# Every tile that the large matmuls read starts at a multiple of 2 KB in SBUF, with a smaller reserve for dynamic DMAs

## The chip, the cores and the metric

The kernel runs on one core of one Trainium2 chip. The metric is the device time of one execution in microseconds; a lower time is better. The time shown is the median of three runs.

## The reference

The reference is one even and one odd layer of an encoder trunk on 512 tokens of 2048 features, in float32, followed by a final RMSNorm. Cut to what matters:

```python
# even layer: one projection, 2048 -> 8192, in eight parts
h = rms_norm(x, g) * (1.0 + scale) + shift            # scale, shift, gate: silu(c) @ w_mod + b_mod
q, k, v, z_a, u_b, g_b, g_c, z_b = split(h @ w_in)
y_a = dilated_mixture_attention(rope(q), rope(k), v) * silu(z_a)   # 8 heads of 128
y_b = g_b * short_conv(g_c * u_b, conv_w) * silu(z_b)
x = x + gate * (concat(y_a, y_b) @ w_out)
# odd layer: 2048 -> 6144
u, v, z = split(h @ w_in)
v = layer_norm(gelu(v))
y = gelu(u) * (w_s @ v + b_s) * silu(z)
x = x + gate * (y @ w_out)
return rms_norm(x, final_g)
```

Nearly all the arithmetic is in four products with weights: 2048 to 8192, 2048 to 2048, 2048 to 6144 and 2048 to 2048, each for 512 tokens.

## The kernel before, in words

Activations lie feature-major: 128 features on the partitions, 512 tokens along the free dimension, so one "page" is 128 x 512 float32, which is 2048 bytes per partition. A product of two float32 operands is made of three float32r matmuls: each operand is split into a high part (a cast to float32r) and a low part (what the cast lost), and `mm3` (lines 209 to 214) adds high x high (L212), high x low (L213) and low x high (L214) into one PSUM bank. In the profile such a line stands as `ps<-moving,stationary`: in `ps<-hh,whi` the moving operand is the activation's high part `hh`, 512 columns, and the stationary one a 128 x 128 piece of the weight's high part `whi`.

There are two ways of use. `fmajor` (L227) makes 128 output features for all tokens: the weights are stationary and the activations `hh`, `lh` move (48 matmuls per output tile). `tmajor` (L249) makes 512 output features for each of four token tiles: pieces of `hh`, `lh` are stationary and the weights `whi`, `wlo` move. `half` (L238) is `fmajor` for 256 tokens, used for the last two output tiles of each output projection. The q k product (`scores`, L412) has the same three matmuls with `hqk`, `lqk` on both sides.

Weights come in slices of 128 x 1024 by DMAs of SyncE's queue (`Stream.ahead`, L183) into `wraw` (three buffers); ScalarE casts a slice to `whi` (L191), VectorE subtracts to `wlo` (L192), two buffers each. A slice feeds 24 matmuls of 512 columns. Up to 180 us the conditioning product `silu(c) @ w_mod` runs on VectorE over 48 tiles (`mod_tile`, L161 to L170) beside the first matmuls.

The order of the work on each engine is that of the program's text as a tile framework schedules it. Tiles come from pools: `const` (allocated first), `work` (all through the kernel: `xy`, `hh`, `R`, `r4`, `tmp`, `wraw`, `whi`, `wlo`, `lh`, `mx`, `den`, laid one after the other), and pools of one phase each (`pm`, `pa`, `pb`, `pw`, `pc`, `pz`) behind it. `r4` (L126), `mx` and `den` (L413, L414) are tiles of 16 bytes per partition with two buffers of 32 bytes each, so `tmp` and what follows lie 64 bytes off the pages ahead of it, and the phase pools another 128 bytes off. The first 16384 bytes of every partition are reserved for dynamic DMAs. What the allocator then gives (bytes in a partition, modulo 512, which is also the length of a stationary piece's row of 128 columns, so that all pieces of a tile share its remainder):

| tiles | read by matmuls as | before: first address, mod 512 | after: first address, mod 512 |
|---|---|---|---|
| `hh` (16) | moving in `fmajor`, stationary in `tmajor` | 52608, 384 | 38912, 0 |
| `lh` (16) | the same | 126400, 448 | 112640, 0 |
| `whi`, `wlo` of `work` (2 + 2) | stationary in `fmajor`, moving in `tmajor` | 110016 and 118208, 448 | 96256 and 104448, 0 |
| `whi`, `wlo` of `pa`, `pw` | the same, up to 200 us and at the change of layers | from 159296, 64 | from 145408, 0 |
| `hqk`, `lqk`, `hpt`, `lpt`, `hv`, `lv` | attention, both sides | from 175680, 64 | from 161792, 0 |
| `p`, `sv`, `wst` | transposes and the odd layer's mixing | from 167488, 64 | from 153600, 0 |
| `ident`, `ones`, `cs` | small matmuls of the norms and transposes | 17376, 17888, 19328: 480, 480, 384 | 2016, 2528, 5440: 480, 480, 320 |

Before, the tiles end at byte 228928; after, at 215040.

Of the kernel before, what the change touches and what calls it, by code (L numbers as in the profile page):

```python
# [9 lines left out]
F32 = mybir.dt.float32  # L10
# [6 lines left out]
P = 128  # L17
KT = D // P
NT = S // P
# [2 lines left out]
EPS = 1e-6  # L22
SCALE = P ** -0.5
HALF = 1024
ALL, LEFT, RIGHT = slice(0, S), slice(0, S // 2), slice(S // 2, S)

# Columns of the packed per-feature vectors.
V_ABB, V_SGB, V_ABG, V_SGG, V_FG, V_CONV, V_LNG, V_LNB, V_C, V_N = 0, 48, 96, 112, 128, 144, 168, 184, 200, 216


def rows(c0):
    """A feature-major tile: 128 columns of a weight, two slices of eight row tiles each."""
    return [[(kt, c0, P) for kt in range(8 * h, 8 * h + 8)] for h in range(2)]


def wide(c0, n):
    """n columns of a weight, row tile after row tile, in slices of 1024 columns."""
    per = HALF // n
    return [[(kt, c0, n) for kt in range(per * i, per * i + per)] for i in range(KT // per)]

# [1 line left out]
A_Q, A_K, A_V, A_Z, B_U, B_GB, B_GC, B_Z = (i * 1024 for i in range(8))  # L42
AB_PLAN = []
W_P = 768
# Columns that are taken while the conditioning arrives, beside the first W_P gates of A.
AB_GROUPS = [
    [(A_V, 512)],
    [(A_Z + W_P, 256), (B_U, P), (B_GC, P)],
# [18 lines left out]
def trunk(ctx, tc, xT, vecs, ab_wm, sg_wm, ab_wp, ab_wg, ab_wi, ab_wo, sg_wi, sg_wo, wsT, bs, rope, band, eye, out):  # L67
    nc = tc.nc
    PS = bass.MemoryType.PSUM
    const = ctx.enter_context(tc.tile_pool(name="const", bufs=1))  # L70
    work = ctx.enter_context(tc.tile_pool(name="work", bufs=2))
# [7 lines left out]
        return (pool or work).tile([P, S], dt, tag=tag, bufs=bufs, name=tag)  # L79

    class Pages:
        """Pages in groups of four, each group one block of memory."""

        def __init__(self):
            self.g = [work.tile([P, 4, S], F32, tag="xy", bufs=4, name="xy") for _ in range(4)]
# [7 lines left out]
    def bank():  # L93
        return psum.tile([P, S], F32, tag="ps", name="ps")

# [1 line left out]
    vec = const.tile([P, V_N], F32, name="vec")  # L97
    pm = tc.alloc_tile_pool(name="pm", bufs=1)
    cb = pm.tile([P, D], F32, name="cb")
# [4 lines left out]
    macc = {n: const.tile([P, 48], F32, name=f"macc_{n}") for n in ("ab", "sg")}  # L104
    gsc = {n: const.tile([P, KT], F32, name=f"gsc_{n}") for n in ("ab", "sg")}

    nc.sync.dma_start(out=vec, in_=vecs)
    nc.sync.dma_start(out=ident, in_=eye)
    x_t = Pages()
# [5 lines left out]
    def v1(c):  # L115
        return vec[:, c:c + 1]

# [1 line left out]
    def rms(parts, cols=ALL):  # L119
        n = (cols.stop - cols.start) // P  # L120
        sums = [bank() for _ in range(n)]
        for j, s in enumerate(parts):
            for i, acc in enumerate(sums):
                ts = slice(cols.start + i * P, cols.start + (i + 1) * P)
                nc.tensor.matmul(acc[:, 0:1], lhsT=s[:, ts], rhs=ones[:, 0:1], start=j == 0, stop=j == len(parts) - 1)  # L125
        r4 = work.tile([P, NT], F32, tag="r4", name="r4")  # L126
        for i, acc in enumerate(sums):
            nc.vector.tensor_scalar(out=r4[:, i:i + 1], in0=acc[:, 0:1], scalar1=1.0 / D, scalar2=EPS, op0=ALU.mult, op1=ALU.add)  # L128
        nc.gpsimd.tensor_tensor(out=r4[:, :n], in0=r4[:, :n], in1=mhalf[:, :n], op=ALU.pow)  # L129
        dg = page("tmp", 4)  # L130
        for i in range(n):
            nc.vector.tensor_scalar(out=dg[:, i * P:(i + 1) * P], in0=ident, scalar1=r4[:, i:i + 1], scalar2=None, op0=ALU.mult)
        return dg
# [9 lines left out]
        nc.scalar.activation(out=sq[:, cols], in_=t[:, cols], func=AF.Square)  # L143
        return sq

# [1 line left out]
    cs = const.tile([P, KT], F32, name="cs")  # L147
    nc.scalar.activation(out=cs, in_=vec[:, V_C:V_C + KT], func=AF.Tanh, scale=0.5)
    nc.vector.scalar_tensor_tensor(out=cs, in0=cs, scalar=1.0, in1=vec[:, V_C:V_C + KT], op0=ALU.add, op1=ALU.mult)
    for i in range(4):  # L150
        acc = bank()
# [23 lines left out]
            out=gsc[n][:, kt:kt + 1], in0=mods[n][:, KT + kt:KT + kt + 1], scalar=1.0, in1=g,  # L175
            op0=ALU.add, op1=ALU.mult)

# [1 line left out]
    class Stream:  # L179
        def __init__(self, src, n):  # L180
            self.src, self.n, self.got, self.at = src, n, {}, 0
# [25 lines left out]
        return hi, lo  # L207

    def mm3(acc, w, m, first, last):
        """acc += w.T m for operands in two parts each; the product of the two low parts is below  # L210
        float32's own rounding of the sum."""
        nc.tensor.matmul(acc, lhsT=w[0], rhs=m[0], start=first, stop=False)  # L212
        nc.tensor.matmul(acc, lhsT=w[0], rhs=m[1], start=False, stop=False)  # L213
        nc.tensor.matmul(acc, lhsT=w[1], rhs=m[0], start=False, stop=last)  # L214
# [10 lines left out]
            return w  # L225

    def fmajor(pos, act):  # L227
        """128 features on partitions, all tokens."""
        acc = bank()
        for h in range(2):  # L230
            hi, lo = pos.slice()
            for k in range(8):
                kt = 8 * h + k
                cs = slice(k * P, (k + 1) * P)
                mm3(acc, (hi[:, cs], lo[:, cs]), act[kt], kt == 0, kt == KT - 1)
        return acc

    def half(parts, act, cols, at=None, meanwhile=None):  # L238
        """A feature-major tile for one half of the tokens."""
        acc = bank()  # L240
        for kt in range(KT):
            hi, lo = parts[kt // 8]
            cs = slice(kt % 8 * P, (kt % 8 + 1) * P)
            mm3(acc[:, cols], (hi[:, cs], lo[:, cs]), (act[kt][0][:, cols], act[kt][1][:, cols]), kt == 0, kt == KT - 1)
            if kt == at:
                meanwhile()
        return acc

    def tmajor(pos, act):  # L249
        """512 features of each token tile, tokens on partitions."""  # L250
        accs = [bank() for _ in range(NT)]
        for i in range(8):
            hi, lo = pos.slice()
            for k in range(2):
                kt = 2 * i + k
                cs = slice(k * S, (k + 1) * S)
                for j, acc in enumerate(accs):
                    ts = slice(j * P, (j + 1) * P)
                    a = act[kt]
                    mm3(acc, (a[0][:, ts], a[1][:, ts]), (hi[:, cs], lo[:, cs]), kt == 0, kt == KT - 1)  # L260
        return accs

    def modulated(n, kt, t, r, to=None, cols=ALL):
        """h = x r g (1 + scale) + shift, in two parts."""
        xr = page("tmp", 4)
        nc.vector.scalar_tensor_tensor(  # L266
            out=xr[:, cols], in0=t[:, cols], scalar=gsc[n][:, kt:kt + 1], in1=r[:, cols], op0=ALU.mult, op1=ALU.mult)
        hi, lo = to or (page("hh", 16, F32R), page("lh", 16, F32R))
        sh = mods[n][:, kt:kt + 1]
        nc.scalar.activation(out=hi[:, cols], in_=xr[:, cols], func=AF.Identity, bias=sh)  # L270
        nc.vector.scalar_tensor_tensor(  # L271
            out=lo[:, cols], in0=xr[:, cols], scalar=sh, in1=hi[:, cols].bitcast(F32), op0=ALU.add, op1=ALU.subtract)
        return hi, lo

    def twice_silu(acc, s):
        """2 silu(z) = (tanh(z/2) + 1) z."""
        nc.scalar.activation(out=s, in_=acc, func=AF.Tanh, scale=0.5)
        nc.vector.scalar_tensor_tensor(out=s, in0=s, scalar=1.0, in1=acc, op0=ALU.add, op1=ALU.mult)
        return s
# [1 line left out]
    s_abi, s_abo = Stream(ab_wi, len(AB_PLAN)), Stream(ab_wo, len(OUT_PLAN))  # L281
    s_sgi, s_sgo = Stream(sg_wi, len(SG_PLAN)), Stream(sg_wo, len(OUT_PLAN))

    # ================= layer 0 =================
    class Later:
        """Conditioning tiles that follow the weights' slices at an even pace."""

        def __init__(self, pool, tiles, slices):
            self.pool, self.tiles, self.step, self.at = pool, tiles, len(tiles) / slices, 0.0
# [14 lines left out]
    h = []  # L304
    pos = Pos(s_abi, s_abo)
    pa = tc.alloc_tile_pool(name="pa", bufs=2, reuse_waits="tile")
    parts = []
# [8 lines left out]
    r0 = page("R", 2)  # L316
    spread(rms(parts[:1]), r0)

    # While the conditioning arrives: the gates of A, half of its values, and what the first head and
    # the first features of B need. Six tiles stay in PSUM; the others are summed in SBUF, quarter of  # L320
    # the features by quarter, four tiles at a time.
    def split_w(src, n, pool, bufs):
        raw = work.tile([P, HALF], F32, tag="wraw", bufs=3, name="wraw")[:, :n]
        size = HALF if pool is work else n
# [7 lines left out]
    gates = [bank() for _ in range(6)]  # L332
    sums, held = {}, {}
# [23 lines left out]
    for kt in range(KT):  # L357
# [11 lines left out]
        if q:  # L369
            at = 4 * (q - 1) + 2 * (i % 2)  # L370
# [39 lines left out]
        return split_to(a, "qk", 2, pb)  # L410

    def scores(q, k):  # L412
        mx = work.tile([P, NT], F32, tag="mx", name="mx")  # L413
        den = work.tile([P, NT], F32, tag="den", name="den")  # L414
        ps = []
        for i in range(NT):
            ts = slice(i * P, (i + 1) * P)
            acc = bank()
# [70 lines left out]
    spill = dram.tile([KT, P, S], F32, name="spill")  # L489

    def project(pos, n, y, src, done, wider, left, more=None):
        """The residual sums, the two last of them by halves of the tokens."""
        yy = [split_to(y[kt], "h", 16) for kt in range(KT)]
        res = Pages()
        for g in range(4):
# [19 lines left out]
        two = [[pos.slice(), pos.slice()] for _ in range(2)]  # L515
# [4 lines left out]
        r = page("R", 2)  # L520
# [9 lines left out]

        return res, r, right

    # The slices that the halves of the tokens go through twice, or far apart.
    h = []

    def done0(f, res):
# [13 lines left out]

    x2, r1, right = project(Pos(s_abo, s_sgi, later), "ab", y, xT, done0, wider0, left0, s_sgi)

    # ================= layer 1 =================
    pos = Pos(s_sgi, s_sgo)
    first = [bank() for _ in range(NT)]
    parts = right()
# [26 lines left out]
    for i in range(2):  # L583
        acc = bank()
# [35 lines left out]
    for f in range(KT):  # L620
        accu = fmajor(pos, h)
        m = mix(f)
# [31 lines left out]


def sliced(w, plan):
    """The slices of a weight in the order of their use, each a block of 128 x 1024."""
    w = w.reshape(KT, P, -1)
    a = np.empty((len(plan), P, HALF), w.dtype)
    for i, parts in enumerate(plan):  # L660
        at = 0
        for kt, c0, n in parts:
            a[i, :, at:at + n] = w[kt, :, c0:c0 + n]
            at += n
    return a
# [61 lines left out]
```

## Time and profile before

| | before |
|---|---|
| median of three runs | 1776.43 us |
| lowest and highest | 1772.96 and 1776.67 us |
| profiled execution, first to last instruction | 1773.5 us |
| TensorE busy | 1719.1 us, 97% |
| VectorE busy | 967.8 us, 55% |
| ScalarE busy | 511.2 us, 29% |
| GpSimd busy | 159.2 us, 9% |
| bytes moved by DMA | 276.10 MB, mean 156 GB/s |

The profiled execution is one of its own; the profile gives its span alone, and the median lies 2.9 us above that. The busy time of TensorE counts a matmul from its start to its modelled end, and consecutive matmuls overlap, so the mean length of a matmul (some 390 ns for 512 columns) is not its cost: in a stream without waits the cost of a matmul is the step from its start to the next one's start. The timeline shows starts to 0.01 us, so a step is read over many matmuls: last start less first start, divided by the count.

### The profile page before, as it was taken

The numbers are of one execution on the slowest core, as the hardware profiler recorded it, in microseconds if no ns is written. First come the engines' busy times: TensorE is split into PE (matmuls) and PEld (weight loads), VectorE is DVE, ScalarE is ACT, GpSimd is POOL, SyncE is SP. The second block draws the span as 40 slices with busy tenths as digits, with TensorE's granted clock in tenths as the row PEclk, the third lists the DMA queues.
The fourth block names the chain that finished last, engine by engine and source line by source line (L and its number), as shares of the span: only waits on it lengthen the run. The fifth ranks groups of instructions, "written<-read, shape, count | busy, mean of one in ns | idle before, by whom it ended". The sixth has DMA issues, their size and how long they took to land.

```text
span 1773.5 us, 19357 instructions
## 1 busy us (share of the span) xinstructions
PE 1719.1 (97%) x7638; PEld 1390.4 (78%) x7638; DVE 967.8 (55%) x1446; ACT 511.2 (29%) x709; POOL 159.2 (9%) x103
## 2 busy tenths in 40 slices
PE   5898999999999999999999999999999999999996
PEld 4677787887888887888888988888888888888885
DVE  7898648565645565657554562226444444453344
ACT  3232234232213232324222432222222122242230
POOL 2574520000000000000000000000000000000002
PEclk7999999999999999999999999999999999999998
DMA  8787444344445444445654522334444434352322
GB/s 307 252 294 258 143 135 132 137 172 156 140 163 189 145 162 159 155 154 188 236 178 171 166 94 74 97 98 135 143 134 140 141 132 142 131 190 95 95 95 95
DMA packets 86971, 276.10 MB, mean 156 GB/s; under 512 B 8800, under 2 KB 13152, under 8 KB 86880
## 3 DMA queue, kind: packets, MB, share of 16 engines
q1 hardware_dynamic: 86880, 274.87, 45.8%
q8 instruction: 59, 0.97, 0.2%
q14 instruction: 32, 0.26, 0.0%
HBM read 266.45 MB, written 8.39 MB: 155 GB/s over the span
## 4 chain that ended last, share of the span: by engine, by line
PE 89%; DVE 8%; issue 2%; ACT 1%; DMA 1%; POOL 0%; SPq 0%; DVEq 0%; POOLq 0%; ACTq 0%
PE ps L212 29%; PE ps L213 29%; PE ps L214 29%; DVE mraw L167 4%; PE ps L610 1%; PE ps L437 1%; DVE gsc_ab L174 1%; DVE lh L271 1%; DVE xy L646 1%; DVE tmp L266 1%; ACT hh L270 0%; DMA mraw<-in_ab_wm_dram 0%; PE ps L125 0%; DMA xy<-in_xT_dram 0%; PE ps L138 0%
## 5 line engine op out<-in xcount | busy, mean ns | idle before, releaser
L212 PE MATMUL ps<-hh,whi 128*128 128x512 f32 (+1 forms) x1984 | 776.7, 393 | 17.0 <-ACT hh L270 12.1
L213 PE MATMUL ps<-lh,whi 128*128 128x512 f32 (+1 forms) x1984 | 778.0, 392 | 0.6 <-DVE lh L271 0.6
L214 PE MATMUL ps<-hh,wlo 128*128 128x512 f32 (+1 forms) x1984 | 768.5, 387 | 1.5 <-POOL wlo L329 1.5
L192 DVE TENSOR_TENSOR wlo<-wraw,whi 128x1024 fp32r<-128x1024 f32 x252 | 308.1, 1224 | 495.1 <-ACT whi L191 439.9
L191 ACT CAST whi<-wraw 128x1024 fp32r<-128x1024 f32 x252 | 264.0, 1049 | 940.6 <-PE ps L213 769.3
L212 PEld LDWEIGHTS ps<-hh,whi 128*128 128x128 f32 x1984 | 373.6, 189 | 110.8 <-ACT hh L270 15.8
L214 PEld LDWEIGHTS ps<-hh,wlo 128*128 128x128 f32 x1984 | 375.4, 189 | 90.2 <-POOL wlo L329 2.3
L213 PEld LDWEIGHTS ps<-lh,whi 128*128 128x128 f32 x1984 | 375.2, 189 | 80.6 <-DVE lh L271 1.4
L212 PE MATMUL ps<-whi,hh 128*128 128x512 f32 x384 | 152.8, 398 | 1.7 <-DVE xy L355 1.6
L213 PE MATMUL ps<-wlo,hh 128*128 128x512 f32 x384 | 150.6, 392 | 0.1
L214 PE MATMUL ps<-whi,lh 128*128 128x512 f32 x384 | 150.3, 391 | 0.0
L167 DVE CUSTOM_DVE_ANT_0 mraw<-mraw,cb,vec 128x1024 f32<-128x1024 f32 x96 | 133.2, 1387 | 30.7 <-DMA mraw<-in_sg_wm_dram 20.1
L329 POOL TENSOR_TENSOR wlo<-wraw,whi 128x512 fp32r<-128x512 f32 (+1 forms) x64 | 119.8, 1894 | 101.1 <-ACT whi L328 99.0
L212 PEld LDWEIGHTS ps<-whi,hh 128*128 128x128 f32 x384 | 72.4, 189 | 19.3 <-DVE xy L355 3.2
L214 PEld LDWEIGHTS ps<-whi,lh 128*128 128x128 f32 x384 | 72.1, 188 | 17.0
L213 PEld LDWEIGHTS ps<-wlo,hh 128*128 128x128 f32 x384 | 72.3, 188 | 16.3 <-POOL wlo L329 0.8
L129 POOL TENSOR_TENSOR r<-r,mhalf 128x2 f32<-128x2 f32 (+1 forms) x5 | 5.7, 1139 | 807.3 <-DVE r L128 807.3
L167 DVE CUSTOM_DVE_ANT_0 mraw<-mraw,cb,macc_ab 128x1024 f32<-128x1024 f32 x48 | 74.3, 1547 | 1.2
L408 POOL TENSOR_TENSOR tmp<-tmp,ropeT 128x512 f32<-128x512 f32 x16 | 20.8, 1302 | 523.5 <-DVE wlo L192 470.5
L328 ACT CAST whi<-wraw 128x512 fp32r<-128x512 f32 (+1 forms) x64 | 42.3, 672 | 86.4 <-DMA wraw<-in_ab_wp_dram 41.5
L167 DVE CUSTOM_DVE_ANT_0 mraw<-mraw,cb,macc_sg 128x1024 f32<-128x1024 f32 x48 | 61.5, 1282 | 3.3 <-DMA mraw<-in_sg_wm_dram 2.0
L501 DVE SCALAR_TENSOR_TENSOR xy<-ps,mod_sg,xy 128x512 f32<-128x512 f32 (+1 forms) x18 | 12.4, 691 | 55.8 <-PE ps L214 55.8
(127 smaller groups left out, 880.0 us busy)
## 6 DMA issues: line engine op xcount, KB each, us to landing
mraw<-in_ab_wm_dram SPq DMA_DIRECT2D x96, 512.0 KB, 4.9
mraw<-in_sg_wm_dram SPq DMA_DIRECT2D x96, 512.0 KB, 5.3
wraw<-in_sg_wi_dram SPq DMA_DIRECT2D x96, 512.0 KB, 3.5
wraw<-in_ab_wi_dram SPq DMA_DIRECT2D x92, 512.0 KB, 3.5
wraw<-in_ab_wo_dram SPq DMA_DIRECT2D x32, 512.0 KB, 3.6
wraw<-in_sg_wo_dram SPq DMA_DIRECT2D x32, 512.0 KB, 3.5
wraw<-in_ab_wg_dram SPq DMA_DIRECT2D x48, 256.0 KB, 2.9
wraw<-in_ab_wp_dram SPq DMA_DIRECT2D x16, 384.0 KB, 4.7
```

The source lines that it names most:

```text
L167: nc.vector.tensor_tensor_reduce(out=raw, in0=raw, in1=cb[:, h * HALF:(h + 1) * HALF], scale=0.5, scalar=v1(b + nt) if h == 0 else macc[n] ...
L174: nc.vector.scalar_tensor_tensor(out=gsc[n][:, kt:kt + 1], in0=mods[n][:, KT + kt:KT + kt + 1], scalar=1.0, in1=g, op0=ALU.add, op1=ALU.mult)
L191: nc.scalar.copy(out=hi, in_=raw)
L192: nc.vector.tensor_tensor(out=lo, in0=raw, in1=hi.bitcast(F32), op=ALU.subtract)
L212: nc.tensor.matmul(acc, lhsT=w[0], rhs=m[0], start=first, stop=False)
L213: nc.tensor.matmul(acc, lhsT=w[0], rhs=m[1], start=False, stop=False)
L214: nc.tensor.matmul(acc, lhsT=w[1], rhs=m[0], start=False, stop=last)
L266: nc.vector.scalar_tensor_tensor(out=xr[:, cols], in0=t[:, cols], scalar=gsc[n][:, kt:kt + 1], in1=r[:, cols], op0=ALU.mult, op1=ALU.mult)
L271: nc.vector.scalar_tensor_tensor(out=lo[:, cols], in0=xr[:, cols], scalar=sh, in1=hi[:, cols].bitcast(F32), op0=ALU.add, op1=ALU.subtract)
L328: nc.scalar.copy(out=hi, in_=raw)
L329: nc.gpsimd.tensor_tensor(out=lo, in0=raw, in1=hi.bitcast(F32), op=ALU.subtract)
L408: nc.gpsimd.tensor_tensor(out=sw, in0=sw, in1=sinT, op=ALU.mult)
```

## The change

It alters where tiles lie, and nothing of what is computed. Three edits do it: the three small tiles `r4`, `mx` and `den` go from `work` to `const`; a tile `pad` of 368 float32 per partition (1472 bytes) closes `const`, so that `work` begins at 6144, a multiple of 2048; and the reserve for dynamic DMAs is given as 1024 bytes where it was 16384. `pad` has one MEMSET of 128 x 1 on GpSimd, since a tile has to be written. The rest of the diff takes out comments and docstrings; line numbers after them are four higher in the changed kernel. On every engine the instructions stand in the same order with the same waits as before, but for that one MEMSET.

```diff
+PAD = 368
...
+    pad = const.tile([P, PAD], F32, name="pad")
+    nc.gpsimd.memset(pad[:, 0:1], 0.0)
     nc.sync.dma_start(out=vec, in_=vecs)
...
-        r4 = work.tile([P, NT], F32, tag="r4", name="r4")
+        r4 = const.tile([P, NT], F32, tag="r4", bufs=2, name="r4")
...
-        mx = work.tile([P, NT], F32, tag="mx", name="mx")
-        den = work.tile([P, NT], F32, tag="den", name="den")
+        mx = const.tile([P, NT], F32, tag="mx", bufs=2, name="mx")
+        den = const.tile([P, NT], F32, tag="den", bufs=2, name="den")
...
-    nc = bacc.Bacc("TRN2", target_bir_lowering=False, num_devices=1)
+    nc = bacc.Bacc("TRN2", target_bir_lowering=False, num_devices=1, dynamic_dma_scratch_size=1024)
```

## Rows read from the trace of the kernel before

**Rows 1.** The page: TensorE's busy row, its granted clock by slices, the chain's shares.

```profile
PE 1719.1 (97%) x7638; PEld 1390.4 (78%) x7638; DVE 967.8 (55%) x1446; ACT 511.2 (29%) x709; POOL 159.2 (9%) x103
...
PEclk7999999999999999999999999999999999999998
...
PE 89%; DVE 8%; issue 2%; ACT 1%; DMA 1%; POOL 0%; SPq 0%; DVEq 0%; POOLq 0%; ACTq 0%
```

**Rows 2.** Busy time by stretches: length; PE, PEld, DVE, ACT, POOL; clock; DMA share; GB/s.

```profile
167.70:172.30 4.60, 4.60 (x12) 3.63 (x11) 3.30 (x6) 0.72 (x1) 0.00 (x0) 0.50 0.96 363
...
200.00:1000.00 800.00, 799.55 (x3513) 644.28 (x3513) 456.56 (x717) 243.30 (x344) 38.90 (x30) 1.00 0.48 162
...
721.13:723.63 2.50, 2.50 (x13) 2.06 (x12) 1.62 (x3) 1.53 (x2) 0.00 (x0) 1.00 0.90 369
...
1200.00:1700.00 500.00, 500.00 (x2202) 403.33 (x2202) 227.42 (x330) 129.91 (x156) 1.84 (x1) 1.00 0.40 133
```

**Rows 3.** Waits: the longest of the weights' path (us in total, times, longest).

```profile
ACT whi L191 <- PE ps L213: 769.3, 185, 5.9
```

**Rows 4.** Matmuls by line and shape, 200 to 1700 us: count, busy us, mean ns.

```profile
L212 PE MATMUL ps<-hh,whi 128*128 128x512 f32 x1663 | 663.1, 399 | 0.0
L213 PE MATMUL ps<-lh,whi 128*128 128x512 f32 x1662 | 661.5, 398 | 0.0
L214 PE MATMUL ps<-hh,wlo 128*128 128x512 f32 x1663 | 652.9, 393 | 0.0
L212 PE MATMUL ps<-whi,hh 128*128 128x512 f32 x336 | 132.8, 395 | 0.0
```

**Rows 5.** TensorE's timeline in `fmajor`: start, length, operation; last row 24 matmuls on.

```profile
605.55 0.40 PE L212 MATMUL ps<-hh,whi 128*128 128x512 f32 x1
605.79 0.40 PE L213 MATMUL ps<-lh,whi 128*128 128x512 f32 x1
606.03 0.39 PE L214 MATMUL ps<-hh,wlo 128*128 128x512 f32 x1
...
611.18 0.40 PE L212 MATMUL ps<-hh,whi 128*128 128x512 f32 x1
```

**Rows 6.** The same in `tmajor`, weights at remainder 448; the rows are 45 matmuls apart.

```profile
1100.23 0.39 PE L212 MATMUL ps<-whi,hh 128*128 128x512 f32 x1
...
1110.53 0.39 PE L212 MATMUL ps<-whi,hh 128*128 128x512 f32 x1
```

**Rows 7.** Token-major matmuls, weights at remainder 64 (`pw`); 12 matmuls apart.

```profile
1051.66 0.40 PE L212 MATMUL ps<-whi,hh 128*128 128x512 f32 x1
...
1054.43 0.40 PE L212 MATMUL ps<-whi,hh 128*128 128x512 f32 x1
```

**Rows 8.** The q k product of one head; first and last of its 12 matmuls.

```profile
721.13 0.39 PE L212 MATMUL ps<-hqk 128*128 128x512 f32 x1
...
723.63 0.40 PE L214 MATMUL ps<-hqk,lqk 128*128 128x512 f32 x1
```

**Rows 9.** The q k product of another head; first and last of its 12 matmuls.

```profile
303.35 0.40 PE L212 MATMUL ps<-hqk 128*128 128x512 f32 x1
...
305.89 0.40 PE L214 MATMUL ps<-hqk,lqk 128*128 128x512 f32 x1
```

**Rows 10.** `fmajor`-shaped matmuls at half the granted clock; 11 matmuls apart.

```profile
167.70 0.63 PE L213 MATMUL ps<-lh,whi 128*128 128x512 f32 x1
...
172.39 0.63 PE L212 MATMUL ps<-hh,whi 128*128 128x512 f32 x1
```

**Rows 11.** `half` (256 columns); the rows are 28 matmuls apart.

```profile
1015.02 0.28 PE L213 MATMUL ps<-lh,whi 128*128 128x256 f32 x1
...
1018.32 0.28 PE L214 MATMUL ps<-hh,wlo 128*128 128x256 f32 x1
```

**Rows 12.** DMA queues of the page: packets, MB, share of 16 engines.

```profile
q1 hardware_dynamic: 86880, 274.87, 45.8%
```

**Rows 13.** The nearest MEMSET of GpSimd: min/median/max ns, start in us.

```profile
L113 POOL MEMSET mhalf<- x1: 105/105/105, 0.7 to 0.7; 128x8 f32 x1
```

## The prediction, made before the changed kernel ran

> **What bounds the kernel now.** I read the page first: its busy row, the clock by slices and the shares of the chain [rows 1]. The reader is to see TensorE at 97%, its clock granted in full in nearly all slices, and 89% of the chain on it. Then the busy time by stretches [rows 2]: from 200 to 1000 us TensorE works 799.55 of 800 us and from 1200 to 1700 us all 500, with VectorE under 60% and the DMAs at 40 to 48%. So from 200 us to the tail the time is the number of matmuls times the step from one start to the next. Before that it is not: in the stretch at 167.7 us VectorE works 3.30 of 4.60 us, the DMAs are at 0.96 and the clock at half. The waits say that the weights are early: ScalarE waited 769.3 us for TensorE to give back `whi` [rows 3].
>
> The step itself comes from the timeline, last start less first start over the count. Feature-major matmuls of 512 columns make 24 steps from 605.55 to 611.18 us, **234.6 ns** each [rows 5]. Token-major ones make 45 steps in 10.30 us, **228.9 ns** [rows 6]; with weights that lie at remainder 64 in place of 448, 12 steps in 2.77 us, 230.8 ns [rows 7]. The q k product makes 11 steps in 2.50 us, **227.3 ns** [rows 8], for another head in 2.54 us, 230.9 ns [rows 9]. All have the same clock, 512 moving columns, one weight load for each matmul and the same three lines; what differs is which tiles they read, thus the addresses. [...] It is not the traffic of DMAs: the faster head ran with the DMAs at 0.90 [rows 2]. My reading is that the moving read and the weight load beside it get in each other's way in SBUF, by an amount that depends on how their addresses stand to each other.
>
> **The change part by part.**
>
> *Feature-major matmuls, 512 columns.* Before, moving tiles lie at 384 (`hh`) and 448 (`lh`) modulo 512 and the weights at 448. After, all are at 0. Of such matmuls the program has 1663 + 1662 + 1663 = 4988 from 200 to 1700 us [rows 4]. The trace has no aligned matmul of this kind. Below, the bound is 213.3 ns (twice the clock of [rows 10]). Above, it is the slowest single step, 0.24 us from 605.79 to 606.03 [rows 5]. The nearest row is the q k product: there both sides lie at remainder 64, so they stand to each other just as all tiles will after the change, and the three lines are the same. Its starts have two digits, so 227.3 may be 226.4 to 228.2; I take 227. That is 7.6 ns less, and 4988 x 7.6 ns = **37.9 us**, all of it on the path.
>
> *Token-major matmuls.* 3 x 336 = 1008 in that stretch [rows 4], from 228.9 to 227 ns: 1008 x 1.9 ns = **1.9 us**. The attention products stay as they are: nothing.
>
> *Halves.* 28 steps in 3.30 us, 117.9 ns [rows 11], for 384 matmuls by the code (two output projections, four times 48). No aligned row; I take the same share as above, 7.6 / 234.6 = 3.2%, or 3.8 ns: **1.5 us**. Between 106.7 ns and no change it is 4.3 us to nothing.
>
> *Restarts.* The slower head [rows 9] has 11 steps at 230.9 ns. I read this as a stream that finds its pace only after a few matmuls, since its relative addresses are those of the faster one. 11 x 3.9 ns = 43 ns, after each break of the stream: eight rounds of transposes, sixteen mixing products and some six norms, 30 x 43 ns = **1.3 us** lost again.
>
> *The first 200 us.* The code has 288 matmuls for the gates and 384 for two groups of features there, beside VectorE's conditioning chain; I cost all of them at nothing. If that cover were thin they would give 672 x 7.6 ns = 5.1 us more.
>
> *The small edits.* The MEMSET of `pad` is one instruction like that of `mhalf`, 105 ns at 0.7 us [rows 13], before GpSimd has anything to do; hidden by the first loads. `r4`, `mx` and `den` keep their two buffers, their order and their waits: nothing. [...] VectorE, ScalarE and the DMAs find their tiles elsewhere too, which could help or harm a few per cent of each; they are covered by TensorE from 200 us on [rows 2], and in the first 200 us 2% either way would be 4 us, which goes to the range.
>
> *What is late next.* TensorE asks for slices 3% sooner; ScalarE's 769 us of waiting [rows 3] is the slack for that.
>
> **The sum:** 37.9 + 1.9 + 1.5 - 1.3 = 40.0 us. The profiled execution has a span of 1773.5 us, which becomes 1733.5; it lies 2.9 us under the median of the runs, 1776.4, from which I forecast **1736 us**.
>
> [...] The rows show steps of 227.3 to 234.6 ns for one form of instruction [rows 5, 8]. [...]
>
> [...]
>
> **The rivals.**
>
> *Nothing changes, 1776 us, chance 0.11.* The pace would hang on the form of the loop (which bank is written, how weights repeat), not on addresses. For it: feature-major and q k product differ in more than addresses, [rows 7] too in how many token tiles share a weight. Against it: the q k product has the three lines and the 512 columns of the rest. To this rival belongs that the change does not do what it says: `ident`, `ones` and `cs` stay off 2 KB, but they are read by small matmuls alone, and the tiles of [rows 4] do move to remainder 0.
>
> *The clash becomes the rule, slower, chance 0.11.* With all tiles at the same remainder, each weight load begins where the moving read begins, and each step could be like the slowest one, 0.24 us: in [rows 5] that is the step in which `lh` and `wlo`, both at 448, are read together. 4988 x 5.4 ns + 1008 x 11.1 ns = 38 us more, 1814 us. It decides from a mean step over 234.6 ns on. Against it: in [rows 8] remainders are equal as well, and the step is the shortest of all.
>
> *Only part goes, chance 0.13.* The stream stays at the pace of the slower head, 230.9 ns [rows 9]: 4988 x 3.7 ns = 18 us, 1758 us. For it: two of the rows of equal remainder differ by 3.6 ns. Against it: I see no reason why a long stream should stay there.
>
> *All of the loss goes, chance 0.10.* Steps of 213.3 ns: 4988 x 21.3 + 1008 x 15.6 + 384 x 11.2 ns = 126 us, 1650 us. For it: [rows 10]. Against it: no row at full clock comes near, and equal remainders alone give 227.
>
> **How the numbers follow.** My forecast, with steps of 226 to 229 ns, has a chance of 0.55, the four rivals 0.11, 0.11, 0.13 and 0.10. The range is to hold 8 in 10: it takes the forecast's cases, the partial one and the nearer half of no change, up to 1775; below it goes about half the way to the full gain, to 1692. A measurement of this kernel can tell about 0.2%, 3.6 us, from no change. Faster by more than that is 0.55 + 0.13 + 0.10 = 0.78, the same 0.11, slower 0.11.
>
> **What would show it.** In the changed kernel's timeline the 24 steps of a feature-major stream take 5.45 us, not 5.63; token-major ones about 227 ns; the number of matmuls in a stretch of 200 us grows by 3%; the first 180 us and the tail after the last matmul keep their length; VectorE's and ScalarE's instructions keep their mean lengths. If the feature-major step is still 234 ns, the relation of addresses is not the cause; if it is 213 to 220, the place of a tile by itself counts, not only how two of them stand to each other; if TensorE has idle time before `whi` or `wlo`, the slices have become the bound.

## The result, and the profile after

| | before | changed |
|---|---|---|
| median (four runs each) | 1776.55 us | 1734.88 us |
| lowest and highest | 1772.96 and 1779.37 us | 1734.76 and 1736.97 us |
| ratio to before, 95% interval | | 0.977, 0.9758 to 0.9782 |
| profiled execution, its own time | | 1734.76 us |
| profiled execution, span | 1773.5 us | 1733.0 us |

The kernel is faster by 2.3%; 1736 us were forecast. The page of the changed kernel first: the busy row, the clock by slices, the shares of the chain, and four of the groups by line (count, busy us, mean ns of one, idle before).

```profile
PE 1676.8 (97%) x7638; PEld 1390.0 (80%) x7638; DVE 969.4 (56%) x1446; ACT 511.7 (30%) x709; POOL 156.2 (9%) x104
...
PEclk7999999999999999999999999999999999999998
...
PE 88%; DVE 7%; issue 2%; DMA 1%; ACT 1%; POOL 0%; SPq 0%; DVEq 0%; POOLq 0%; ACTq 0%
...
L216 PE MATMUL ps<-hh,whi 128*128 128x512 f32 (+1 forms) x1984 | 761.4, 386 | 18.3 <-ACT hh L274 14.3
...
L196 DVE TENSOR_TENSOR wlo<-wraw,whi 128x1024 fp32r<-128x1024 f32 x252 | 308.2, 1224 | 469.7 <-ACT whi L195 420.7
L195 ACT CAST whi<-wraw 128x1024 fp32r<-128x1024 f32 x252 | 265.1, 1053 | 905.1 <-PE ps L217 743.6
```

Against [rows 1] the counts are the same but for one more instruction on GpSimd, TensorE is as full as before (97%), its clock is granted as before (mean 0.985 in both), and its busy time is 42 us shorter. VectorE's and ScalarE's work on the weights is not: 1224 and 1053 ns now, 1224 and 1049 ns on the page of before. So TensorE does the same work in less time; the busy time of the other engines changed by 3 us at most. The same stretches as in [rows 2] (length; PE, PEld, DVE, ACT, POOL with counts; clock; DMA share; GB/s):

```profile
200.00:1000.00 800.00, 799.34 (x3680) 664.75 (x3679) 469.94 (x744) 254.24 (x362) 40.05 (x31) 1.00 0.49 166
...
1200.00:1700.00 500.00, 500.00 (x2309) 417.95 (x2308) 223.91 (x315) 137.55 (x165) 0.00 (x0) 1.00 0.40 133
```

In 800 us there are 3680 matmuls where there were 3513, in 500 us 2309 where there were 2202: 4.8% more each, where the prediction named 3% as its sign. Part of that is that the stretches now reach further into the program, with other shapes in them. The step itself is in TensorE's timeline, pairs of rows that are 24 matmuls apart in `fmajor`, 45 in `tmajor`, 11 in the q k product and 28 in `half` (start us, length, operation):

```profile
300.57 0.39 PE L216 MATMUL ps<-hqk 128*128 128x512 f32 x1
...
303.06 0.39 PE L218 MATMUL ps<-hqk,lqk 128*128 128x512 f32 x1
...
600.01 0.39 PE L216 MATMUL ps<-hh,whi 128*128 128x512 f32 x1
...
605.45 0.39 PE L216 MATMUL ps<-hh,whi 128*128 128x512 f32 x1
...
972.33 0.28 PE L217 MATMUL ps<-lh,whi 128*128 128x256 f32 x1
...
975.68 0.28 PE L218 MATMUL ps<-hh,wlo 128*128 128x256 f32 x1
...
1090.23 0.39 PE L216 MATMUL ps<-whi,hh 128*128 128x512 f32 x1
...
1100.43 0.39 PE L216 MATMUL ps<-whi,hh 128*128 128x512 f32 x1
```

Feature-major matmuls step by 5.44 / 24 = 226.7 ns, where [rows 5] had 234.6. Token-major ones step by 10.20 / 45 = 226.7 ns, [rows 6] had 228.9. The q k product of the head that was slow in [rows 9] steps by 2.49 / 11 = 226.4 ns. All three agree now. Half of the 426.4 ns of [rows 10], which stood at a granted clock of 0.50, is 213.2 ns, an estimate of the same step at full clock if it goes with the clock alone; 226.7 ns are 13.5 ns above it. The halves went the other way: 3.35 / 28 = 119.6 ns, [rows 11] had 117.9.

Both kernels issue the same matmuls in the same order, so the steps between starts can be added up by kind over the same instructions (those from 200 us on in the kernel before; sums from both traces):

| kind | count | before, us | changed, us | difference | forecast |
|---|---|---|---|---|---|
| feature-major, 512 columns | 5112 | 1199.2 | 1162.2 | -37.1 | -37.9 |
| token-major, 512 columns | 1008 | 232.0 | 229.4 | -2.7 | -1.9 |
| halves, 256 columns | 384 | 45.9 | 46.6 | +0.7 | -1.5 |
| attention, 512 columns | 192 | 45.3 | 45.6 | +0.3 | 0 |
| small float32 matmuls | 299 | 38.6 | 38.2 | -0.4 | 0 |
| all before 200 us | 642 | 196.2 | 195.9 | -0.3 | 0 |

### The profile page after: what moved, and what is told of

Read it like the earlier page. It is cut to its first block, busy times and chain, and to the rows that moved or that the text cites. A ratio compares the mean times of both kernels' runs of the same rounds, so it can differ in the third digit from the quotient of the medians.

```text
span 1733.0 us, 19358 instructions
## 1 busy us (share of the span) xinstructions
PE 1676.8 (97%) x7638; PEld 1390.0 (80%) x7638; DVE 969.4 (56%) x1446; ACT 511.7 (30%) x709; POOL 156.2 (9%) x104
## 2 busy tenths in 40 slices
DMA packets 86971, 276.10 MB, mean 159 GB/s; under 512 B 8800, under 2 KB 13152, under 8 KB 86880
## 3 DMA queue, kind: packets, MB, share of 16 engines
q1 hardware_dynamic: 86880, 274.87, 46.8%
## 4 chain that ended last, share of the span: by engine, by line
PE 88%; DVE 7%; issue 2%; DMA 1%; ACT 1%; POOL 0%; SPq 0%; DVEq 0%; POOLq 0%; ACTq 0%
PE ps L216 29%; PE ps L218 29%; PE ps L217 29%; DVE mraw L171 4%; PE ps L441 1%; PE ps L614 1%; DVE gsc_ab L178 1%; DVE lh L275 1%; DVE xy L650 1%; DMA xy<-in_xT_dram 1%; ACT hh L274 0%; DVE sv L608 0%; DVE tmp L270 0%; DMA wraw<-in_ab_wp_dram 0%; PE ps L129 0%
## 5 line engine op out<-in xcount | busy, mean ns | idle before, releaser
L216 PE MATMUL ps<-hh,whi 128*128 128x512 f32 (+1 forms) x1984 | 761.4, 386 | 18.3 <-ACT hh L274 14.3
L217 PE MATMUL ps<-lh,whi 128*128 128x512 f32 (+1 forms) x1984 | 762.8, 384 | 0.3 <-DVE lh L275 0.3
L196 DVE TENSOR_TENSOR wlo<-wraw,whi 128x1024 fp32r<-128x1024 f32 x252 | 308.2, 1224 | 469.7 <-ACT whi L195 420.7
L195 ACT CAST whi<-wraw 128x1024 fp32r<-128x1024 f32 x252 | 265.1, 1053 | 905.1 <-PE ps L217 743.6
L171 DVE CUSTOM_DVE_ANT_0 mraw<-mraw,cb,macc_ab 128x1024 f32<-128x1024 f32 x48 | 78.1, 1626 | 1.0
```

The source lines that it names most:

```text
L171: nc.vector.tensor_tensor_reduce(out=raw, in0=raw, in1=cb[:, h * HALF:(h + 1) * HALF], scale=0.5, scalar=v1(b + nt) if h == 0 else macc[n] ...
L195: nc.scalar.copy(out=hi, in_=raw)
L196: nc.vector.tensor_tensor(out=lo, in0=raw, in1=hi.bitcast(F32), op=ALU.subtract)
```

## The experiments

Theory 1: what counts is the **difference** of the start addresses of the two tiles that a matmul reads, the moving and the stationary one. Theory 2: each tile must itself start at a good address (a multiple of 2 KB, as the change has it, or at least of 128 bytes). Theory 3: the smaller reserve, or where memory ends, does it.

**Only the small tiles moved.** The kernel before, with three lines of the change; no pad, the old reserve. All tiles of the large matmuls then lie at remainder 64 modulo 512 (`hh`, `lh`, `whi`, `wlo` and the attention's tiles at 1600 modulo 2048).

```diff
-        r4 = work.tile([P, NT], F32, tag="r4", name="r4")
+        r4 = const.tile([P, NT], F32, tag="r4", bufs=2, name="r4")
-        mx = work.tile([P, NT], F32, tag="mx", name="mx")
-        den = work.tile([P, NT], F32, tag="den", name="den")
+        mx = const.tile([P, NT], F32, tag="mx", bufs=2, name="mx")
+        den = const.tile([P, NT], F32, tag="den", bufs=2, name="den")
```

> Of the change only the move of r4, mx and den out of work: all tiles of the large matmuls then lie at remainder 64 modulo 512, none at a multiple of 2 KB, and the reserve stays 16384 bytes. Theory 1 (the difference between the remainders of the moving and the stationary tile sets the loss): the whole gain, feature-major step 226.7 ns, some 1735 us. Theory 2 (a tile must itself start at a multiple of 2 KB, or at least of 128): steps stay above 230 ns, 1755 to 1776 us. Theory 3 (the reserve or the extent of memory matters): 1776 us.

Measured: 1735.52 us, ratio 0.9776 (0.9758 to 0.9793), the whole gain. Its timeline, 24 steps of `fmajor`:

```profile
604.77 0.39 PE L212 MATMUL ps<-hh,whi 128*128 128x512 f32 x1
...
610.21 0.39 PE L212 MATMUL ps<-hh,whi 128*128 128x512 f32 x1
```

5.44 us, 226.7 ns, with none of these tiles at a multiple of 2 KB, nor of 128 bytes. Theories 2 and 3 fall here: neither the multiple of 2 KB nor the reserve is needed.

**Only pad and reserve.** The changed kernel with the three small tiles back in `work` and a pad that still puts the first tile of `work` at 6144. `hh` is at 0, `lh` and the weights at 64.

```diff
-PAD = 368
+PAD = 416
-        r4 = const.tile([P, NT], F32, tag="r4", bufs=2, name="r4")
+        r4 = work.tile([P, NT], F32, tag="r4", name="r4")
-        mx = const.tile([P, NT], F32, tag="mx", bufs=2, name="mx")
-        den = const.tile([P, NT], F32, tag="den", bufs=2, name="den")
+        mx = work.tile([P, NT], F32, tag="mx", name="mx")
+        den = work.tile([P, NT], F32, tag="den", name="den")
```

> The other part alone: small reserve and a pad that puts the first tiles of work at a multiple of 2 KB, with r4, mx and den left in work, so that hh is at 0, lh and the weights at 64, the phase pools at 192. The differences between tiles are those of the kernel before. Theory 1: nothing gained, feature-major step 234.4 ns, 1776 us. Theory 2: hh is aligned, so two of three matmuls gain: some 1750 us. Theory 3: 1735 us.

Measured: 1774.83 us, ratio 0.9991 (0.9981 to 1.0). 24 steps of `fmajor`:

```profile
604.97 0.40 PE L216 MATMUL ps<-hh,whi 128*128 128x512 f32 x1
...
610.60 0.40 PE L216 MATMUL ps<-hh,whi 128*128 128x512 f32 x1
```

5.63 us, to the digit that of [rows 5], though `hh` now starts at a multiple of 2 KB. The whole of the change's gain is in the three small tiles that no longer stand between the pages.

**How the loss depends on the difference.** The changed kernel with gaps in `work` that move `whi` and `wlo` of that pool up by D bytes and bring `lh` and what follows back to remainder 0 (D in multiples of 32; finer steps were not tried); the diff leaves out a third gap, which is of 0 bytes. In `fmajor` the stationary tile then lies D ahead of the moving one, in `tmajor` D behind. The weights of `pa` and `pw`, and attention, stay at 0.

```diff
+    gaps = {"whi": D, "lh": -D % 512}
+
+    def gap(name):
+        n = gaps.pop(name, 0)
+        if n:
+            nc.gpsimd.memset(work.tile([P, n // 4], F32, tag="gap_" + name, bufs=1, name="gap_" + name)[:, 0:1], 0.0)
...
         raw = work.tile([P, HALF], F32, tag="wraw", bufs=3, name="wraw")[:, :n]
+        gap("whi")
...
+        gap("lh")
         hi, lo = to or (page("hh", 16, F32R), page("lh", 16, F32R))
```

> The changed kernel with the weights of work moved 64 bytes up, hh and lh both at 0: stationary 64 ahead of the moving tile in fmajor, 64 behind in tmajor. Theory 1: a loss of its own size; in the kernel before, two of three matmuls had this difference and the mean step was 234.4 ns, so 234 to 240 ns in fmajor and 1775 to 1800 us. Theory 2 (only the weights are misplaced): the moving tiles are aligned in fmajor, so the step stays near 227 ns there and rises in tmajor, some 1738 us.

> The same with the weights 256 bytes up, half of the span of a weight piece's row. Theory 1 leaves the size open: if the loss grows with the distance, over 234 ns in fmajor; if it is a clash that a distance avoids, under 226.7 ns, down to 213.3 ns, 1650 to 1735 us. Theory 2: as for 64 bytes, 1735 to 1740 us.

> The changed kernel with the weights of work 128 bytes up. [...] Theory 1a (the loss repeats every 128 bytes): 226.7 ns in both, 1735 to 1738 us. Theory 1b (it repeats every 256 bytes): 128 is the far point, and the step may be either side, 213 to 240 ns, the same in fmajor and tmajor; 1660 to 1800 us. Theory 1c (equal remainders are the best there can be): 1735 us or more.

> The weights of work 192 bytes up. Theory 1b (period 256): 192 is -64, so fmajor takes the 228.9 ns that tmajor had at -64, tmajor the 233.3 ns that fmajor had at +64: some 1748 us. Theory 1a (period 128): as at +64, fmajor 233.3, tmajor 228.9 ns, 1771 us.

> The weights of work 32 bytes up, so off the 64 byte grid that every tile had so far. If the loss goes with the distance, between 226.7 and 233.3 ns in fmajor, 1735 to 1771 us; if it goes by blocks of 64 bytes, 226.7 or 233.3 ns and nothing between; if the grid itself matters, over 233.3 ns.

> The weights of work 96 bytes up. By blocks of 64 bytes: the step of the block, as at 64 or at 128 bytes. If the loss goes with the distance: between the steps at 64 and at 128. Over 234 ns if the 64 byte grid itself matters.

Measured, one run each beside kernels before at 1775 to 1776 us: D = 32 gave 1773.62 us, 64 gave 1770.98, 96 gave 1778.33, 128 gave 1767.92, 192 gave 1753.96, 256 gave 1737.37. Single runs tell the order of these medians only roughly; the steps tell more. From the timelines, pairs of rows 24 steps apart, `fmajor` first, then `tmajor`. D = 32, 5.60 us in `fmajor`:

```profile
605.10 0.40 PE L216 MATMUL ps<-hh,whi 128*128 128x512 f32 x1
...
610.70 0.40 PE L216 MATMUL ps<-hh,whi 128*128 128x512 f32 x1
```

D = 64, 5.60 and 5.49 us:

```profile
605.08 0.40 PE L216 MATMUL ps<-hh,whi 128*128 128x512 f32 x1
...
610.68 0.40 PE L216 MATMUL ps<-hh,whi 128*128 128x512 f32 x1
...
1099.84 0.39 PE L216 MATMUL ps<-whi,hh 128*128 128x512 f32 x1
...
1105.33 0.39 PE L216 MATMUL ps<-whi,hh 128*128 128x512 f32 x1
```

D = 192, 5.49 and 5.60 us, the two values changed places (the `fmajor` rows are from 130 us; the stretch at 605 us is one of the few that stood at another pace, see below):

```profile
129.94 0.39 PE L216 MATMUL ps<-hh,whi 128*128 128x512 f32 x1
...
135.43 0.39 PE L216 MATMUL ps<-hh,whi 128*128 128x512 f32 x1
...
1100.06 0.39 PE L216 MATMUL ps<-whi,hh 128*128 128x512 f32 x1
...
1105.66 0.39 PE L216 MATMUL ps<-whi,hh 128*128 128x512 f32 x1
```

D = 128, 5.58 and 5.57 us:

```profile
605.23 0.40 PE L216 MATMUL ps<-hh,whi 128*128 128x512 f32 x1
...
610.81 0.39 PE L216 MATMUL ps<-hh,whi 128*128 128x512 f32 x1
...
1099.92 0.40 PE L216 MATMUL ps<-whi,hh 128*128 128x512 f32 x1
...
1105.49 0.39 PE L216 MATMUL ps<-whi,hh 128*128 128x512 f32 x1
```

D = 256, 5.44 us:

```profile
604.85 0.39 PE L216 MATMUL ps<-hh,whi 128*128 128x512 f32 x1
...
610.29 0.39 PE L216 MATMUL ps<-hh,whi 128*128 128x512 f32 x1
```

Over all stretches of 12 matmuls without a break, the median step (ns) by the start of the stationary tile less that of the moving one, modulo 256:

| difference, bytes | read in | step, 512 columns |
|---|---|---|
| 0 | changed kernel; D = 256 | 226.7 |
| 32 | `fmajor` at D = 32 | 233.3 |
| 64 | `fmajor` at 64, `tmajor` at 192 | 233.3, 233.3 |
| 96 | `fmajor` at 96 | 234.2 |
| 128 | `fmajor` and `tmajor` at 128 | 232.6, 232.6 |
| 160 | `tmajor` at 96 | 233.3 |
| 192 | `fmajor` at 192, `tmajor` at 64 | 228.9, 228.9 |
| 224 | `tmajor` at 32 | 233.3 |

Each of the measured pairs that a period of 256 bytes makes equal is equal: 0 and 256 (226.7 ns), 64 and -192 (233.3), -64 and 192 (228.9), 128 and -128 (232.6). Periods of 128 bytes (0 and 128: 226.7 and 232.6 ns) and of 64 or 32 (0 and 64, 0 and 32: 226.7 and 233.3 ns) are out. Of the eight differences in the table, 0 is the best for 512 columns (226.7 ns, the others 228.9 to 234.2), so none of them as one difference for all tiles gives more than the change did; other mixtures than those of the kernel before were not tried. The loss does not grow with the distance either: 32 bytes cost as much as 64 (233.3 ns).

The table holds for streams that have one difference throughout. In the kernel before, differences alternate in `fmajor` (64, 0 and 64 for L212, L213 and L214), and there the matmul with difference 0 is the slowest of the three: the median steps to the next start, from 200 us on, are 235, 237 and 231 ns. The three take 703 ns together, and the table would add up to 693. So a matmul's step hangs on its neighbours too, and the table is no price list for single matmuls.

Some things did not fit what was written. For D = 64 theory 1 had 234 to 240 ns and at least 1775 us; the step is 233.3 ns, the time 1770.98 us. For D = 192 some 1748 us were written, and 1753.96 came. For D = 96 a step over 234 ns was the sign that the 64-byte grid itself matters; 234.2 came in `fmajor`, but 233.3 in `tmajor` and at D = 32, also off that grid, so the sign tells nothing. For D = 256 a distance might have avoided the clash, down to 213.3 ns; it is the same as no distance, 226.7 ns. And at D = 192 some streams of `fmajor` stood at 233.3 ns and not 228.9 (some 7% of them), in two stretches of some 30 and 40 us, so one difference can have two paces that last.

**The halves at another difference.** With 256 columns the order is another: 120.0 ns at difference 0 and 113.3 ns at 192 (medians; D = 192, its `half` streams). So the weights of the last projection's halves, most of which have a pool of their own, were moved by 192 bytes.

```diff
         s_sgo.extra = range(28, 32)
+        nc.gpsimd.memset(s_sgo.pool.tile([P, 48], F32, tag="gap", bufs=1, name="gap")[:, 0:1], 0.0)
```

> The changed kernel with the weights of the last output projection's halves (pool pz) 192 bytes up, the difference at which 256 columns took 113.3 ns and not 120.0. 192 such matmuls x 6.7 ns = 1.3 us less, some 1733.6 us, 0.07%: to be seen in the timeline of that stretch (1.3 us in some 23), hardly in the median. If the difference acts only through long streams, no change.

> The changed kernel as it is, for the comparison with pz192 on one chip: 1735 us.

Measured: 1736.32 us (ratio to before 0.9781, 0.9768 to 0.9795) for the one, 1737.74 us (0.9789, 0.9776 to 0.9802) for the changed kernel beside it; these intervals overlap almost wholly, so no difference is told. (The changed kernel's gain is 2.1% in this comparison and 2.3% in the first; its interval here reaches past 0.98.) In the traces the 192 steps of that stretch take 22.65 us, not 23.29: 0.6 us, half of what was expected. 48 of the matmuls read a slice from `work`, still at 0. The other 144 stood at 113.3 ns until the small matmuls of a norm broke the stream, and at 117.8 ns after that, though the difference was 192 all along. Two pairs of rows, 30 steps apart, 3.40 and 3.53 us:

```profile
1694.65 0.28 PE L216 MATMUL ps<-hh,whi 128*128 128x256 f32 x1
...
1698.05 0.28 PE L216 MATMUL ps<-hh,whi 128*128 128x256 f32 x1
...
1706.83 0.28 PE L218 MATMUL ps<-hh,wlo 128*128 128x256 f32 x1
...
1710.36 0.28 PE L218 MATMUL ps<-hh,wlo 128*128 128x256 f32 x1
```

## Why the prediction was right

*The bound.* The forecast took the step between starts, not the length of a matmul, as the price, and multiplied by counts. That held: from 200 us on the sums by kind give -39.2 us, and the span became 40.5 us shorter. (The rest is a first matmul 0.6 us earlier, 0.3 us before 200 us and 0.5 us behind the last matmul.) That the total of 40.0 us came so close is in part luck: the halves came 2.2 us and feature-major 0.8 us worse than forecast, token-major came 0.8 us better, and of the 1.3 us for restarts 1.0 us did not come.

*Feature-major.* The value was taken from the q k product, because there both sides had equal remainders: 227 ns, and 226.7 came. The prediction had 4988 such matmuls and a base of 234.6 ns from one stretch; over 5112 the mean of before was 234.6 too (waits included), and -37.1 us against -37.9. That the q k product was the right row is shown by the first experiment: equal remainders make the step, 226.7 ns at 64 as at 0.

*Token-major.* -2.7 against -1.9 us: the step of [rows 6] was taken for all, while those with weights in `pw` [rows 7] had 230.8 ns and gained more.

*Halves.* The one step that failed: "I take the same share as above, 3.2%" gave -1.5 us, and +0.7 came. The loss does not go with the columns. Taken against a half and a quarter of the 426.4 ns of [rows 10], 213.2 and 106.6 ns as estimates for 512 and 256 columns at full clock, equal remainders leave about the same for each matmul: 13.5 ns with 512 columns (226.7) and 13.4 with 256 (120.0). The old remainders happened to suit 256 columns better (117.9 ns). The 213.3 and 106.7 ns of the prediction's bounds are estimates of that kind too, and no run shows such a pace: the least medians read here are 226.7 ns with 512 columns and 113.3 with 256. The term was small, 1.5 us of 40, so the forecast survived it.

*Restarts.* 1.3 us were set aside for streams that find their pace slowly, as in [rows 9]. In the changed kernel the q k products after the first, which has a wait in it, run at 226.7 ns from the first matmul on; attention cost 0.3 us more in all. The slow start comes with the stream ahead: where the experiments keep attention at 0 and put the feature-major stream ahead of it at another difference, the same products have mean steps of 226.6 to 230.9 ns, and with that stream at 0 none is over 226.7 (the first apart in both).

*The first 200 us, the MEMSET, the reserve, the small tiles, the other engines:* nothing was forecast, and -0.3 us came before 200 us. (The prediction places 672 feature-major matmuls there; in the timeline of the kernel before it is 456, beside 144 token-major ones. Since they were costed at nothing, this changes no sum.) For the reserve, the first experiment has 16384 bytes and 1735.52 us, the changed kernel 1024 bytes and 1734.88 us; before and after the change 274.87 of 276.10 MB went through the one queue of [rows 12]. The weights stayed early: ScalarE still waits 743.6 us for `whi` against 769.3 [rows 3].

*The rivals.* "Nothing changes" falls with the first experiment: same order of work, same loops, another pace (226.7 ns, not 234.6). "The clash becomes the rule" falls by the step: equal starts are the best of the eight differences (226.7 ns). Its sign in [rows 5], the slow step of `lh` with `wlo`, was read rightly (237 ns), but it belongs to the mixed stream and not to equal starts as such. "Only part goes" does not come: long streams stand at 226.7 ns and not at 230.9. "All of the loss goes" does not come: no stream of 512 columns here, all in float32r, came under 226.6 ns, where that rival had 213.3. With one difference throughout, the step lies between 226.7 and 234.2 ns by the addresses of the two operands.

What is shown is the dependence on the difference of the two tiles' starts, and that this dependence is the whole gain. That it comes from the moving read and the weight load meeting in SBUF is the author's reading that fits it, and it is not shown. The trace of the kernel before shows the two beside each other, the load of `wlo` for the next matmul starting with the matmul of `lh` and `whi`:

```profile
605.79 0.40 PE L213 MATMUL ps<-lh,whi 128*128 128x512 f32 x1
605.79 0.19 PEld L214 LDWEIGHTS ps<-hh,wlo 128*128 128x128 f32 x1
```

Which of the loads (that of this matmul or the next one's) meets which read was not separated, and why the step at difference 0 is 226.7 ns and not the estimated 213.2 stays open.

## What to carry to other kernels

When TensorE is busy without a gap, measure the step from start to start for each kind of matmul and compare kinds with the same number of columns: if they differ, look at the addresses of the two operands. For float32r matmuls of 128 x 128 pieces and 512 columns, as here, let all moving and stationary tiles start at the same remainder modulo 256 bytes (226.7 ns a step here, against 228.9 to 234.2 at the seven other differences tried); here three small tiles between large ones were enough to spoil it (234.6 ns), and moving them elsewhere was the whole remedy. For other column counts another difference can be better (with 256 columns 113.3 ns at 192 and 120.0 at 0 here): measure it.

## What the runs showed that was not expected

The remedy needs no multiple of 2 KB, no pad and no smaller reserve: with every large tile 64 bytes past a multiple of 512 the time was 1735.52 us. The dependence repeats after 256 bytes (226.7 ns at 0 and at 256) and is not symmetric (228.9 ns at 192, 233.3 at 64). At difference 0 a matmul takes 13.4 ns over the estimate from [rows 10] with 256 columns (120.0 ns) and 13.5 with 512 (226.7). In a stream of mixed differences the matmul with difference 0 was the slowest (237 ns). And one difference can have two lasting paces: at D = 192 streams of one kind stood at 228.9 ns in most places and at 233.3 in some, and the halves went from 113.3 to 117.8 ns at a break. What picks the pace stays open.
